# Layer norm without scale or shift: GpSimd's twelve first tiles written as six in a loop, with a semaphore for each operation

## The chip, the cores and the metric

The kernel runs on one core of a Trainium2 chip. The metric is the device time of one execution in microseconds (us). The span of the trace, from the first to the last instruction, is about 2 us shorter than that time; the difference is called "outside the span". All runs shown are in the fast state, on one core with a granted clock of 1.0.

## The reference

```python
# x: 32 x 512 x 1024 float32, eps = 1e-5
mean = np.mean(x, axis=-1, keepdims=True)
var = np.var(x, axis=-1, keepdims=True)
return ((x - mean) / np.sqrt(var + eps)).astype(np.float32)
```

There are 16,384 rows of 1024 elements: 67.11 MB are read and 67.11 MB are written.

## The kernel before

Rows are taken in 17 tiles. A tile has 128 partitions with 8 rows each (4 MiB); the last two have 6 and 2 rows. Six tiles fit into a ring in SBUF. For each tile, four engines hand on to each other:

1. SyncE loads the tile, once the store of the tile six places earlier has freed the slot.
2. VectorE computes statistics (`bn_stats`, 16 instructions for a tile) and raises `taken`.
3. GpSimd merges them in nine small operations into a sum of squares.
4. ScalarE takes the root. VectorE takes the reciprocal of the root. GpSimd multiplies mean and reciprocal.
5. ScalarE normalizes the eight rows in place and issues the store.

VectorE's program and GpSimd's, before:

```python
    def vector(t, arrived, turn):
        K, row, at = plan[t]
        for k in range(K):
            for s in range(NSUB):
                i = nc.vector.bn_stats(...)                    # cut: operands
                if k == 0 and s == 0:
                    i._wait_ge(landed[t], arrived)
                # cut: tile 0 comes in two halves; a wait for the second
        i.then_inc(taken, 1)
        if t >= len(plan) - LAST:                              # LAST = 2
            return
        nc.vector.reciprocal(
            out=rstd[:, at : at + K], in_=std[:, at : at + K]
        )._wait_ge(rooted[t], turn).then_inc(inverse, 1)
    # tiles 0 to 2, then two turns of a loop of six tiles, then the rest

    def gp(i, sem, value):
        nonlocal npool
        i._wait_ge(sem, value).then_inc(pool, 1)
        npool += 1
        return pool, npool

    for t, (K, row, at) in enumerate(plan):
        n = gp(g.tensor_tensor(out=h, in0=mean4[:, :, 0:2], in1=mean4[:, :, 2:4], op=ALU.add), taken, t + 1)
        n = gp(g.tensor_tensor(out=nm, in0=h[:, :, 0], in1=h[:, :, 1], op=ALU.add), *n)
        n = gp(g.tensor_scalar(out=nm, in0=nm, scalar1=-1.0 / H, scalar2=None, op0=ALU.mult), *n)
        # cut: six more, each waiting for the one before it
        if t < len(plan) - LAST:
            n = inverse, t + 1
        else:
            n = gp(g.tensor_tensor(..., op=ALU.pow), rooted[t], 1)
        ready.append(gp(g.tensor_mul(out=nmr[:, at : at + K], in0=nm, in1=rstd[:, at : at + K]), *n))
```

Note the order on VectorE: statistics of tile t, then the reciprocal of tile t, then the statistics of tile t+1. The reciprocal waits for GpSimd and ScalarE.

## Time and profile before

| | before |
|---|---|
| time, median of the first 3 runs | 318.22 us (318.08 to 318.25) |
| span of the profiled run | 315.8 us |
| busy: VectorE, ScalarE, GpSimd | 50%, 48%, 13% |
| bytes moved, rate over the span | 134.2 MB, 425 GB/s |

In the profile, PE, DVE, ACT, POOL and SP are the tensor, vector, scalar, GpSimd and sync engines; L118 is a line of the kernel. In lists in order of time the columns are start, duration, engine, line, operation, out<-in, count; the bracket gives the idle time ahead and what ended it. The slices are 40 equal parts of the span, each digit a busy share in tenths. The lines themselves are in the prediction.

### The profile page before, as it was taken

To read this page: it belongs to the slowest core of one execution; us is meant where nothing else is said; L and a number is where in the kernel's file an instruction comes from. 1 tells how busy PE (TensorE), PEld (TensorE's weight loads), DVE (VectorE), ACT (ScalarE), POOL (GpSimd) and SP (SyncE) were. 2 spreads that over 40 slices of the span, in tenths; PEclk is the share of its full clock that TensorE was granted. 3 is DMA by queue.
4 is the path that set the end of the run, shared out by engine and by line. 5 is a ranking of instruction groups with operands and counts; after the bars stand their busy time and mean duration, and the time that the engine had idled before them with its cause. 6 is when DMAs were issued, how large, how long until landed. Compare 5 with 4: busy or idle time off the path is not lost.

```text
span 315.8 us, 695 instructions
## 1 busy us (share of the span) xinstructions
DVE 156.4 (50%) x273; ACT 153.0 (48%) x146; POOL 41.7 (13%) x176
## 2 busy tenths in 40 slices
DVE  0396595865190752908438093470925619193000
ACT  1006595865925609165190742907438083474700
POOL 0002202022002020020201102011020200205200
DMA  7999999999999999999999999999999999999996
GB/s 299 432 465 398 448 398 415 453 411 452 412 449 415 444 419 452 415 452 415 452 415 448 423 440 432 432 436 432 440 423 440 423 438 432 423 431 447 419 436 295
DMA packets 5044, 134.24 MB, mean 425 GB/s; under 512 B 561, under 2 KB 561, under 8 KB 561
## 3 DMA queue, kind: packets, MB, share of 16 engines
q10 hardware_dynamic: 2592, 69.21, 51.0%
q1 hardware_dynamic: 2448, 65.01, 48.0%
q14 instruction: 4, 0.02, 0.0%
HBM read 67.11 MB, written 67.11 MB: 425 GB/s over the span
## 4 chain that ended last, share of the span: by engine, by line
DMA 61%; DVE 18%; ACT 9%; POOL 5%; issue 2%; ACTq 0%; DVEq 0%; SPq 0%
DMA ring<-in_x_dram 31%; DMA out_dram<-ring 29%; DVE stats L118 17%; ACT ring L228 9%; ACT std L218 1%; POOL rstd L198 1%; POOL dev L179 1%; POOL dev L184 1%; POOL dev L172 0%; POOL dev L177 0%; POOL nmean L168 0%; POOL half L162 0%; POOL half L185 0%; POOL nmean L166 0%; POOL ss L188 0%
## 5 line engine op out<-in xcount | busy, mean ns | idle before, releaser
L118 DVE BATCH_NORM_STATS2 stats<-ring 128x6 f32<-128x512 f32 x256 | 153.4, 677 | 85.4 <-DMA ring<-in_x_dram 84.8
L228 ACT ACTIVATE ring<-ring,nmr,rstd 128x1024 f32<-128x1024 f32 x128 | 146.6, 1226 | 11.2 <-POOL nmr L209 11.2
L218 ACT ACTIVATE std<-ss,eps_t 128x8 f32<-128x8 f32 (+2 forms) x17 | 5.1, 300 | 134.4 <-POOL ss L188 134.0
L162 POOL TENSOR_TENSOR half<-stats 128x16 f32<-128x16 f32 (+2 forms) x17 | 4.0, 234 | 231.6 <-DVE stats L118 231.6
L129 DVE RECIPROCAL rstd<-std 128x8 f32<-128x8 f32 x15 | 3.0, 203 | 48.5 <-ACT std L218 48.5
L179 POOL TENSOR_SCALAR dev<-dev 128x32 f32<-128x32 f32 (+2 forms) x17 | 5.0, 295 | 1.5
L209 POOL TENSOR_TENSOR nmr<-nmean,rstd 128x8 f32<-128x8 f32 (+2 forms) x17 | 3.5, 205 | 9.9 <-DVE rstd L129 9.7
L184 POOL TENSOR_TENSOR dev<-dev,stats 128x32 f32<-128x32 f32 (+2 forms) x17 | 4.3, 255 | 1.4
L172 POOL TENSOR_TENSOR dev<-stats,nmean 128x32 f32<-128x32 f32 (+2 forms) x17 | 4.1, 241 | 1.4
L177 POOL TENSOR_TENSOR dev<-dev 128x32 f32<-128x32 f32 (+2 forms) x17 | 4.0, 238 | 1.3
L168 POOL TENSOR_SCALAR nmean<-nmean 128x8 f32<-128x8 f32 (+2 forms) x17 | 4.0, 235 | 1.5
L185 POOL TENSOR_TENSOR half<-dev 128x16 f32<-128x16 f32 (+2 forms) x17 | 3.7, 215 | 1.3
L166 POOL TENSOR_TENSOR nmean<-half 128x8 f32<-128x8 f32 (+2 forms) x17 | 3.4, 202 | 1.3
L188 POOL TENSOR_TENSOR ss<-half 128x8 f32<-128x8 f32 (+2 forms) x17 | 3.4, 201 | 1.3
L198 POOL TENSOR_TENSOR rstd<-std,power 128x6 f32<-128x6 f32 (+1 forms) x2 | 2.1, 1041 | 3.0 <-ACT std L218 3.0
L218 ACT ACT_TABLE_LOAD x1 | 1.3, 1283 | 1.3 <-SPq L54 1.3
L133 DVE MEMSET eps_t<- 128x1 f32 x1 | 0.1, 59 | 1.0 <-SPq L54 1.0
L264 POOL MEMSET const-float32-0.0<- 128x1 f32 x1 | 0.1, 99 | 0.2 <-issue 0.2
L264 POOL MEMSET const-bfloat16-1.0<- 128x1 bf16 x1 | 0.1, 102 | 0.0
L264 POOL MEMSET const-uint8-127<- 128x1 uint8 x1 | 0.1, 102 | 0.0
L264 POOL MEMSET const-float32-1.0<- 128x1 f32 x1 | 0.1, 99 | 0.0
L134 DVE MEMSET power<- 128x8 f32 x1 | 0.1, 65 | 0.0
## 6 DMA issues: line engine op xcount, KB each, us to landing
out_dram<-ring ACTq DMA_DIRECT2D x15, 4096.0 KB, 47.4
ring<-in_x_dram SPq DMA_DIRECT2D x14, 4096.0 KB, 44.4
ring<-in_x_dram SPq DMA_DIRECT2D x1, 3072.0 KB, 42.0
out_dram<-ring ACTq DMA_DIRECT2D x1, 3072.0 KB, 16.5
ring<-in_x_dram ACTq DMA_DIRECT2D x1, 2048.0 KB, 12.2
ring<-in_x_dram SPq DMA_DIRECT2D x1, 2048.0 KB, 12.4
ring<-in_x_dram SPq DMA_DIRECT2D x1, 1024.0 KB, 53.8
out_dram<-ring ACTq DMA_DIRECT2D x1, 1024.0 KB, 14.8
```

The costliest lines, as they stand in the source:

```text
L118: i = nc.vector.bn_stats(out=stats[:, at + k, s, :], in_=ring[:, at + k, s * BN_MAX : (s + 1) * BN_MAX],)
L162: g.tensor_tensor(out=h, in0=mean4[:, :, 0:2], in1=mean4[:, :, 2:4], op=ALU.add),
L168: g.tensor_scalar(out=nm, in0=nm, scalar1=-1.0 / H, scalar2=None, op0=ALU.mult),
L172: g.tensor_tensor(out=d, in0=mean4, in1=nm.unsqueeze(2).to_broadcast([P, K, H]), op=ALU.add),
L177: n = gp(g.tensor_mul(out=d, in0=d, in1=d), *n)
L179: g.tensor_scalar(out=d, in0=d, scalar1=float(D // H), scalar2=None, op0=ALU.mult),
L184: n = gp(g.tensor_tensor(out=d, in0=d, in1=m2, op=ALU.add), *n)
L185: n = gp(g.tensor_tensor(out=h, in0=d[:, :, 0:2], in1=d[:, :, 2:4], op=ALU.add), *n)
L198: g.tensor_tensor(out=rstd[:, at : at + K], in0=std[:, at : at + K], in1=power[:, :K], op=ALU.pow,),
L209: g.tensor_mul(out=nmr[:, at : at + K], in0=nm, in1=rstd[:, at : at + K]),
L218: nc.scalar.activation(out=std[:, at : at + K], in_=ss[:, at : at + K], func=AF.Sqrt, bias=eps_t[:], scale=1.0 / D,)._wait_ge(*summed[t]). ...
L228: i = nc.scalar.activation(out=ring[:, k, :], in_=ring[:, k, :], func=AF.Identity, bias=nmr[:, k : k + 1], scale=rstd[:, k : k + 1],).then ...
```

## The change

The intent is a shorter program for GpSimd: tiles 0 to 5 are written once and run twice, and tiles 12 to 16 follow unrolled. A wait in a loop needs a value that holds in each turn. One semaphore that counts all operations does not give it simply, so each operation has its own, which rises by one per tile, and a register holds the tile's number.

```diff
-    taken, inverse, pool, act = map(
-        nc.alloc_semaphore, ("taken", "inverse", "pool", "act")
-    )
+    taken, inverse, act = map(nc.alloc_semaphore, ("taken", "inverse", "act"))
+
+    steps = [nc.alloc_semaphore(f"step_{i}") for i in range(11)]
 ... (cut)
-    for t, (K, row, at) in enumerate(plan):
+    def combine(t, count):
 ... (cut)
+        before = taken
+        def then(step, i, other=None):
+            nonlocal before
+            i._wait_ge(before, count) if other is None else i._wait_ge(*other)
+            before = steps[step]
+            i.then_inc(before, 1)
+
+        then(0, g.tensor_tensor(out=h, in0=mean4[:, :, 0:2], in1=mean4[:, :, 2:4], op=ALU.add))
 ... (cut: the same ten operations, eleven on the last two tiles)
+    count = g.alloc_register("count")
+    g.reg_mov(count, 1)
+    with g.Fori(0, TURNS):
+        for t in range(SLOTS):
+            combine(t, count)
+            g.reg_add(count, count, 1)
+    for t in range(TURNS * SLOTS, len(plan)):
+        combine(t, t + 1)
+    summed = [(steps[8], t + 1) for t in range(len(plan))]
+    ready = [(steps[10], t + 1) for t in range(len(plan))]
```

By my listing of the two programs, GpSimd goes from 183 instructions to 131.

More of the change, by code (lines that the diff above doesn't have):

```diff
@@ L145 @@
         vector(t, 16, 1)
-    npool, summed, ready = 0, [], []
-    def gp(i, sem, value):
-        nonlocal npool
-        i._wait_ge(sem, value).then_inc(pool, 1)
-        npool += 1
-        return pool, npool
     g = nc.gpsimd
-    for t, (K, row, at) in enumerate(plan):
+    def combine(t, count):
+        K, row, at = plan[t]
         parts = stats[:, at : at + K].rearrange("p g s (h c) -> p g (s h) c", h=2)
@@ L160 @@
         nm, d, h = nmean[:, at : at + K], dev[:, :K], half[:, :K]
-        n = gp(
-            g.tensor_tensor(out=h, in0=mean4[:, :, 0:2], in1=mean4[:, :, 2:4], op=ALU.add),
-            taken,
-            t + 1,
-        )
-        n = gp(g.tensor_tensor(out=nm, in0=h[:, :, 0], in1=h[:, :, 1], op=ALU.add), *n)
-        n = gp(
-            g.tensor_scalar(out=nm, in0=nm, scalar1=-1.0 / H, scalar2=None, op0=ALU.mult),
-            *n,
-        )
-        n = gp(
-            g.tensor_tensor(
-                out=d, in0=mean4, in1=nm.unsqueeze(2).to_broadcast([P, K, H]), op=ALU.add
-            ),
-            *n,
-        )
-        n = gp(g.tensor_mul(out=d, in0=d, in1=d), *n)
-        n = gp(
+        s2, r, std_t = ss[:, at : at + K], rstd[:, at : at + K], std[:, at : at + K]
+        before = taken
[5 more added lines that the diff above has]
+        then(0, g.tensor_tensor(out=h, in0=mean4[:, :, 0:2], in1=mean4[:, :, 2:4], op=ALU.add))
+        then(1, g.tensor_tensor(out=nm, in0=h[:, :, 0], in1=h[:, :, 1], op=ALU.add))
+        then(
+            2,
+            g.tensor_scalar(out=nm, in0=nm, scalar1=-1.0 / H, scalar2=None, op0=ALU.mult),
+        )
+        spread = nm.unsqueeze(2).to_broadcast([P, K, H])
+        then(3, g.tensor_tensor(out=d, in0=mean4, in1=spread, op=ALU.add))
+        then(4, g.tensor_mul(out=d, in0=d, in1=d))
+        then(
+            5,
             g.tensor_scalar(
@@ L181 @@
             ),
-            *n,
         )
-        n = gp(g.tensor_tensor(out=d, in0=d, in1=m2, op=ALU.add), *n)
-        n = gp(g.tensor_tensor(out=h, in0=d[:, :, 0:2], in1=d[:, :, 2:4], op=ALU.add), *n)
-        summed.append(
-            gp(
-                g.tensor_tensor(
-                    out=ss[:, at : at + K], in0=h[:, :, 0], in1=h[:, :, 1], op=ALU.add
-                ),
-                *n,
-            )
-        )
+        then(6, g.tensor_tensor(out=d, in0=d, in1=m2, op=ALU.add))
+        then(7, g.tensor_tensor(out=h, in0=d[:, :, 0:2], in1=d[:, :, 2:4], op=ALU.add))
+        then(8, g.tensor_tensor(out=s2, in0=h[:, :, 0], in1=h[:, :, 1], op=ALU.add))
         if t < len(plan) - LAST:
-            n = inverse, t + 1
+            own = inverse, count
         else:
-            n = gp(
-                g.tensor_tensor(
-                    out=rstd[:, at : at + K],
-                    in0=std[:, at : at + K],
-                    in1=power[:, :K],
-                    op=ALU.pow,
-                ),
-                rooted[t],
-                1,
-            )
-        ready.append(
-            gp(
-                g.tensor_mul(
-                    out=nmr[:, at : at + K], in0=nm, in1=rstd[:, at : at + K]
-                ),
-                *n,
-            )
-        )
+            i = g.tensor_tensor(out=r, in0=std_t, in1=power[:, :K], op=ALU.pow)
+            then(9, i, (rooted[t], 1))
+            own = steps[9], t - (len(plan) - LAST) + 1
+        then(10, g.tensor_mul(out=nmr[:, at : at + K], in0=nm, in1=r), own)
+    count = g.alloc_register("count")
[8 more added lines that the diff above has]
+    ready = [(steps[10], t + 1) for t in range(len(plan))]
     for t, (K, row, at) in enumerate(plan):
```

## The prediction

The six parts are 0 us each, and the sum is 318.22 + 0 = 318.2 us. The 0.005 for a faster result is the author's estimate alone.

> **What bounds the kernel now.** I read the page first: the busy shares of the engines, then the slices, then the DMA totals and issues.
>
> ```profile
> DVE 156.4 (50%) x273; ACT 153.0 (48%) x146; POOL 41.7 (13%) x176
> ...
> DMA  7999999999999999999999999999999999999996
> ...
> q14 instruction: 4, 0.02, 0.0%
> HBM read 67.11 MB, written 67.11 MB: 425 GB/s over the span
> ...
> out_dram<-ring ACTq DMA_DIRECT2D x15, 4096.0 KB, 47.4
> ring<-in_x_dram SPq DMA_DIRECT2D x14, 4096.0 KB, 44.4
> ```
>
> What to see: no engine is above 50%, and the sixteen DMA engines are at 90% or more in 38 of 40 slices; only the first and the last are lower (7 and 6 tenths). So 134.2 MB of transfers set the time, and GpSimd, which the change is about, is at 13%. The last two rows show how deep the transfers queue: a 4 MiB store takes 47.4 us from issue to landing, a load 44.4 us.
>
> Next, the Vector engine in order of time, for the pace of the steady part:
>
> ```profile
> 85.53 9.59 DVE L118 BATCH_NORM_STATS2 stats<-ring 128x6 f32<-128x512 f32 x16 [6.34 <-DMA ring<-in_x_dram]
> 98.36 0.20 DVE L129 RECIPROCAL rstd<-std 128x8 f32<-128x8 f32 x1 [3.24 <-ACT std L218]
> 104.89 9.59 DVE L118 BATCH_NORM_STATS2 stats<-ring 128x6 f32<-128x512 f32 x16 [6.33 <-DMA ring<-in_x_dram]
> ```
>
> A tile takes 104.89 - 85.53 = 19.36 us, and in each VectorE sits 6.3 us waiting for the next load. One tile is a load and a store of 4.19 MB each: 8.39 MB / 19.36 us = 433 GB/s. GpSimd's own waits, and the one in front of tile 6, say the same from its side:
>
> ```profile
> POOL half L162 <- DVE stats L118: 231.6, 17, 22.6
> ...
> 114.56 0.23 POOL L162 TENSOR_TENSOR half<-stats 128x16 f32<-128x16 f32 x1 [15.72 <-DVE stats L118]
> ```
>
> GpSimd waits 231.6 of 315.8 us for statistics. The chain of waits does pass through it, but look at what carries the chain: 61% of it is DMA, 5% POOL, and the two DMA pieces in a row are the whole latency of a queue, not of one transfer.
>
> ```profile
> 66.06 9.17 ACT ring L228 x8
> 75.23 0.02 issue
> 75.25 43.33 DMA out_dram<-ring
> 118.58 0.02 issue
> 118.60 44.36 DMA ring<-in_x_dram
> ```
>
> **The slack of a GpSimd delay.** This is the number that decides, so I work it out. With loads and stores sharing 433 GB/s, one 4.19 MB transfer moves in about 19.4 us (estimate: 4.19 MB at half of 433). The store above took 43.33 us and the load 44.36 us, so each stood some 24 us in a queue behind others. A store that is issued later by d us therefore waits d us less in the queue, as long as d stays under about 24 us; the DMA engines do not notice. The ring closes the same way: 9.6 (statistics) + 3.6 (GpSimd, root, reciprocal, last multiply) + 9.2 (ACT) + 43.3 + 44.4 is 110 us on this path, against six tiles of 19.36 = 116 us, and most of both DMA terms is queueing.
>
> [...]
> - [...] the new code keeps a wait at each step, only on a semaphore of its own. In the trace each such wait shows as 0.07 to 0.08 us of issue between two GpSimd pieces of the chain.
> - [...] The trace has a loop already, on VectorE; going into it left 0.6 us of idle in all (moves, an alignment, branches)[...].
> - [...] the page of before shows what fetches cost in any case: 4 packets, 0.02 MB, 0.0% of the engines.
>
> **The change, part by part.** By the listing of both programs GpSimd goes from 183 instructions to 131 (tiles 0 to 5 written once and run twice, tiles 6 to 11 gone, tiles 12 to 16 as they were). Other engines keep theirs in the same order; only the semaphore names on ACT's two waits per tile change. What GpSimd executes on data is unchanged: the same 10 operations on each of 15 tiles and 11 on each of the last two.
>
> 1. *Removed:* 60 instructions of code [...], no executed work. [...] 0 us.
> 2. *Waits.* For 12 tiles the value comes from a register instead of a constant. VectorE has the same change inside one run, between its reciprocals ahead of the loop (constant) and in it (register):
>
> ```profile
> 39.02 0.02 issue
> 39.04 0.20 DVE rstd L129
> ...
> 65.52 0.02 issue
> 65.54 0.21 DVE rstd L129
> ```
>
> Both waits end 0.02 us after the releaser, so a register costs nothing to see there. For GpSimd I take 0; if it were 0.1 us for each of 10 waits, that is 1 us a tile, against 24 us of slack.
> 3. *Counter:* one register addition a tile. VectorE's sequencer pieces in its loop entry last 0.04 us each; 12 x 0.04 = 0.5 us in all, behind the last multiply of a tile, where GpSimd next waits 9 to 16 us for statistics. On the path: 0.
> 4. *Entry, one branch back, one exit.* By VectorE's entry some 0.6 us each. The entry lies in the first 22.6 us, in which GpSimd waits for tile 0. The branch back lies after tile 5's last multiply, in the 15.72 us shown above. The exit lies after tile 11, in an equal gap. On the path: 0.
> 5. *Semaphores:* one (`pool`) becomes eleven, each counted by one operation alone. More names, the same number of increments: 0.
> 6. *Start and tail.* The first store is issued at 35.85 us; until then 25.2 MB of loads for six slots are queued, some 58 us of DMA work at 433 GB/s, so a delay of the first tiles is hidden too. Tiles 15 and 16 end the program and are outside the loop, with constants as before.
>
> Sum on the path that sets the end: 0 us. 318.22 + 0 = **318.2 us**.
>
> **Rivals.**
> - *GpSimd gets slow enough to starve the stores.* It would need about 24 us more per looped tile, on an engine that works 2.4 us on one (41.7 / 17). A register wait would have to cost over 2 us. Speaking for it: nothing in this trace shows a register wait on GpSimd itself. Against: VectorE's 0.02 us. If it happened, each of 12 tiles would add its excess over the slack, and the time would go to 330 us or more. I give it 1%.
> - *The smaller program saves time* (fewer instruction fetches among saturated queues, or less to do around the span). For: the time of the profiled run is 318.03 and its span 315.8, so 2.2 us lie outside it, and instructions are fetched by the same DMA engines. Against: four packets in a whole span. It could give 0.1 to 0.3 us, far under 2%.
> [...]
> - *The order of loads and stores in the queues shifts*, since stores are issued slightly later. The bytes and the rate stay; it moves the end by tenths of a us in either direction. This sets my range.
>
> **Range and chances.** The three runs of before lie within 0.17 us, the profiled one at 318.03. I allow four times that spread each way for another order in the queues and another build: 317.5 to 318.9. Two per cent is 6.4 us; only the first rival makes that, so slower has 0.01. Faster by 6.4 us would need 134.2 MB in under 309.6 us of span, 434 GB/s on average with the fill and drain included[...]: 0.005.
>
> **What would show it.** Right: DMA slices all 9 but the ends, tiles still 19.36 us apart on VectorE, GpSimd's operations with the same means (about 0.2 to 0.3 us), idle before `half` still ended by the statistics. Step 2 shows in the issue gaps between GpSimd pieces of looped tiles (0.07 us if free) against those of tiles 12 to 16; steps 3 and 4 in a first operation of a tile that starts later than 0.07 us after the last statistics; step 1 in the instruction queue's packets. The prediction is wrong if VectorE's 6.3 us waits for loads shrink or vanish in the loop, or if a slice of DMA in the middle falls under 9.

## The result

| | before | after |
|---|---|---|
| median of 6 runs each | 318.24 us (318.08 to 318.44) | 317.77 us (317.60 to 318.24) |
| ratio after / before | | 0.9986, 95% interval 0.9973 to 0.9999 |
| span | 315.8 us (profiled run) | 315.8 to 316.4 us (6 runs) |
| outside the span | 2.2 us (profiled run) | 1.80 to 1.88 us (6 runs) |

The ratio is the mean time of one kernel's fast runs over that of the other's of the same rounds, so it is not quite the ratio of the medians. The difference is 0.14%. The two spans are alike: what difference there is lies outside.

The page of the kernel after, in the lines that answer to those of before (busy shares, DMA slices, instruction queue, bytes):

```profile
DVE 156.4 (49%) x273; ACT 153.0 (48%) x146; POOL 41.7 (13%) x176
...
DMA  7999999999999999999999999999999999999996
...
q14 instruction: 3, 0.02, 0.0%
HBM read 67.11 MB, written 67.11 MB: 425 GB/s over the span
```

The DMA slices are the same, digit for digit, and GpSimd is busy for the same 41.7 us with the same 176 instructions that count as work. The instruction queue has 3 packets against 4 in the span, but this is no saving: by the records of the two traces, three packets of 8,192 bytes fall within the span in both, and the fourth of before has 24 bytes and stands at 0.02 us.

VectorE's statistics of tiles 5 and 6 after, and GpSimd's first operation on tile 6, which is the first after the branch back:

```profile
86.32 9.59 DVE L119 BATCH_NORM_STATS2 stats<-ring 128x6 f32<-128x512 f32 x16 [6.35 <-DMA ring<-in_x_dram]
105.66 9.59 DVE L119 BATCH_NORM_STATS2 stats<-ring 128x6 f32<-128x512 f32 x16 [6.30 <-DMA ring<-in_x_dram]
```

```profile
115.33 0.23 POOL L166 TENSOR_TENSOR half<-stats 128x16 f32<-128x16 f32 x1 [15.69 <-DVE stats L119]
```

A tile takes 105.66 - 86.32 = 19.34 us (19.36 before), and VectorE still waits 6.3 us for each load. The statistics of tile 6 end at 105.66 + 9.59 = 115.25 us, and GpSimd starts 0.08 us later; before, it was 114.56 - 114.48 = 0.08 us as well. So the branch back is hidden in the 15.69 us of idle time: its record stands at 99.48 us, and two short `MODIFY_POOL_CONFIG` records at the head of the loop, which the second turn runs again, are over at 99.83 us. The record of this branch is 0.05 us long, that of the exit after tile 11 0.04 us. No packet of the instruction queue starts between 94.3 us and the end of the span, so no fetch shows for the branch either.

The end of the chain's passage through GpSimd on tile 3, after:

```profile
65.34 0.07 issue
65.41 0.20 POOL ss L183
65.61 0.61 issue
66.23 0.03 POOLq L197
66.26 0.00 issue
66.26 0.21 POOL nmr L190
```

The gap ahead of an operation that waits on the register's value is 0.07 us, what it was with a constant. The counter's addition is the piece of 0.03 us on GpSimd's sequencer (`POOLq`; 0.05 us on tile 0). It stands ahead of the last multiply in time, although it comes after it in the program: it starts 0.04 us after the end of the reciprocal for which the multiply waits, and the multiply starts 0.08 us after that end, on the twelve tiles with an addition as on tiles 12 to 14 without one. The multiply starts 0.65 us after the last sum (66.26 - 65.61), as before (65.82 - 65.17). So the addition costs nothing either.

### The profile page after: what moved, and what is told of

It is laid out like the page before. It is cut to its first block, busy times and chain, and to the rows that moved or that the text cites. A ratio compares the mean times of both kernels' runs of the same rounds, so it can differ in the third digit from the quotient of the medians.

```text
span 316.0 us, 713 instructions
## 1 busy us (share of the span) xinstructions
DVE 156.4 (49%) x273; ACT 153.0 (48%) x146; POOL 41.7 (13%) x176
## 4 chain that ended last, share of the span: by engine, by line
DMA 61%; DVE 18%; ACT 9%; POOL 5%; issue 2%; ACTq 0%; DVEq 0%; POOLq 0%; SPq 0%
DMA ring<-in_x_dram 32%; DMA out_dram<-ring 29%; DVE stats L119 17%; ACT ring L215 9%; POOL rstd L187 1%; POOL dev L177 1%; POOL dev L181 1%; ACT std L205 0%; POOL dev L173 0%; POOL nmean L170 0%; POOL dev L174 0%; POOL half L166 0%; POOL half L182 0%; POOL nmean L167 0%; POOL ss L183 0%
```

## The experiments

Two questions were open. First: 0.47 us between the medians is small, but is it real, and where does it come from? Second: the prediction rests on a slack of 24 us for a delay on GpSimd. The result does not test that, since the change brought no delay to hide.

### Why 0.4 us less?

The changed kernel's own loop has a scalar multiplication that waits on a register. To keep clear of that form of instruction, in the experiments the two scalar multiplications are `tensor_tensor` with constant tiles. VectorE fills these in two more memsets. All outputs were correct.

**r1_loop** is the changed kernel so rewritten:

```diff
-        then(2, g.tensor_scalar(out=nm, in0=nm, scalar1=-1.0 / H, scalar2=None, op0=ALU.mult))
+        then(2, g.tensor_tensor(out=nm, in0=nm, in1=minus[:, :K], op=ALU.mult))
 ... (cut)
-        then(5, g.tensor_scalar(out=d, in0=d, scalar1=float(D // H), scalar2=None, op0=ALU.mult))
+        then(5, g.tensor_tensor(out=d, in0=d, in1=wide[:, :K], op=ALU.mult))
```

> The loop with the two scalar multiplications of GpSimd as tensor_tensor with a constant tile (131 GpSimd instructions, as in the change). Theory 'less code': 0.3 to 0.5 us under the kernel before (about 317.8 against 318.24), with a span that is equal within 0.2 us, so the gain lies outside the span (some 1.8 us outside instead of 2.2) and one 8 KB instruction packet fewer after the end. Theory 'noise or another order in the queues': within 0.2 us of before, the part outside the span at 2.2 us. Either way the gaps between GpSimd operations stay 0.07 to 0.08 us.

**r2_unrolled** is r1_loop without the loop:

```diff
-    with g.Fori(0, TURNS): ... (cut)
+    for t in range(len(plan)):
+        combine(t, t + 1)
```

> The same with its eleven semaphores but all 17 tiles written out (183 GpSimd instructions, as before). Theory 'less code': equal to before within 0.15 us, 2.2 us outside the span. Theory 'the separate semaphores are what gains': about 317.8, like the loop.

**r3_loop_pad** is r1_loop and **r4_before_pad** the kernel before, with 52 and 128 memsets of one column ahead of GpSimd's work:

```diff
+    for i in range(52):                                  # 128 in r4_before_pad
+        nc.gpsimd.memset(pad[:, i : i + 1], 0.0)
```

> The loop with 52 small memsets ahead of it on GpSimd, in its first idle 22 us, so that the program has 183 GpSimd instructions again. Theory 'less code': the gain is gone, about 318.2, 2.2 us outside the span. Theory 'it is the loop itself': about 317.8.

> The kernel before with 128 small memsets ahead of GpSimd's work [...]. Theory 'less code, step by instruction packet': 0.3 to 0.5 us slower than before, outside the span. Theory 'only a fixed boundary that the change went under': equal to before within 0.15 us. In no case is the span more than 0.3 us longer, since the memsets run in GpSimd's first idle 22 us.

These four ran on one chip with five rounds. Their numbers are in the table below. The loop repeats the result (317.77 us against 318.17, ratio 0.9988, interval 0.9975 to 1.0002), and the part outside the span, which varies by at most 0.09 us between the runs of a kernel (spans are recorded to 0.1 us), tells where: 1.79 to 1.87 us against 2.19 to 2.27, with mean spans of 315.94 and 315.93 us. The separate semaphores are not the cause: r2_unrolled has them and 2.20 to 2.26 us outside.

Nor is it the amount of code, which I had expected. r3_loop_pad has as many instructions as before by the listing (one more by the trace) and still 1.82 to 1.87 us outside. r4_before_pad has 128 more and no more outside than before (2.17 to 2.20). A delay experiment that is told further down, d5_late, gave a hint: 195 unrolled GpSimd instructions and 1.77 to 1.86 us outside. In the traces of before and after, the large packets of the instruction queue have 8,192 bytes. So the next idea was that the place counts where GpSimd's program ends within such a packet.

**e2_before_pad12** and **e3_before_pad76** are the kernel before with 12 and 76 of these memsets. That makes 195 instructions, as in d5_late, and 259, which is 128 more than the changed kernel has. How many instructions fill a packet no trace shows; that programs 128 apart end at the same place in one was the author's assumption:

> The kernel before with 12 small memsets in GpSimd's first idle time: 195 GpSimd instructions, as many as d5_late has. The time outside the span was 1.8 us in d5_late and 2.2 us in before. Theory 'where GpSimd's program ends in its 8 KB instruction packets decides' (P): 1.8 us outside, so about 317.8. Theory 'it is the late work itself, or the loop' (W): 2.2 us outside, 318.2.

> With 76 memsets: 259 GpSimd instructions[...]. Theory P: 1.8 us outside the span, about 317.8, though the program is the longer. Theory W or 'less code': 2.2 us or more outside, 318.2.

**e4_pow_pad** puts 125 of them into p0_pow (below), in which VectorE's program is shorter too, and has 323, again 128 more than d5_late:

> The kernel p0_pow (198 GpSimd instructions, 2.2 us outside) with 125 memsets: 323[...]. Theory P: 1.8 us outside the span. If VectorE's program, shorter here by its reciprocals, decides as well: 2.2 us.

| kernel | loop on GpSimd | GpSimd instructions | median, us | mean span, us | outside, us |
|---|---|---|---|---|---|
| before (of r1 to r4) | no | 183 | 318.17 | 315.93 | 2.19 to 2.27 |
| after | yes | 131 | 317.77 | 315.98 | 1.80 to 1.88 |
| r1_loop | yes | 131 | 317.77 | 315.94 | 1.79 to 1.87 |
| r2_unrolled | no | 183 | 318.30 | 316.12 | 2.20 to 2.26 |
| r3_loop_pad | yes | 183 | 317.95 | 316.20 | 1.82 to 1.87 |
| r4_before_pad | no | 311 | 318.27 | 316.08 | 2.17 to 2.20 |
| e2_before_pad12 | no | 195 | 317.92 | 316.10 | 1.80 to 1.85 |
| e3_before_pad76 | no | 259 | 317.80 | 316.05 | 1.77 to 1.85 |
| d5_late | no | 195 | 317.97 | 316.07 | 1.77 to 1.86 |
| p0_pow (VectorE shorter) | no | 198 | 318.20 | 316.00 | 2.15 to 2.24 |
| e4_pow_pad (VectorE shorter) | no | 323 | 318.76 | 316.60 | 2.15 to 2.24 |

The part outside the span takes one of two values 0.4 us apart. Two experiments say that the amount of code is not what chooses between them: e3_before_pad76 has 76 instructions more than before and is on the lower value, and r4_before_pad with 52 more than that is on the higher one. With the other engines' programs as they were and without a loop on GpSimd, 183 and 311 instructions give 2.2 us, 195 and 259 give 1.8 us, as expected. e1_late8 and d10_late, with the 195 of d5_late (and, like it, two more memsets on VectorE), have 1.82 to 1.86 and 1.79 to 1.84 us. The 183 and 311 are 128 apart, and so are the changed kernel's 131 and the 259. That is all that speaks for a place within a packet; these are only four lengths without a loop, and that the packet is the cause is not shown. But the same 0.4 us can be had by adding twelve idle memsets.

What this account does not cover stays open. r3_loop_pad has the 183 of before by the listing and 1.85 us. It may be that a loop moves something; but by the trace its program is one instruction longer than that of before (197 records against 196, the loop counted once), and no kernel without a loop was tried between 183 and 195, so the border may lie between the two. e4_pow_pad is 128 longer than the 195 of d5_late and has 2.2 us (and, unexplained, a span 0.6 us longer than before). There VectorE's program is shorter too, as in p0_pow and p10_pow_late (2.14 to 2.23 us outside), and whether its end counts too was not tried alone. What the core does in these 0.4 us no trace shows: the records of instructions stop at the end of the span. The packets of 8,192 bytes that come after it don't settle it. In the profiled runs there is one in every kernel that has the lower value, r3_loop_pad excepted. There are two in before, r2_unrolled and r4_before_pad, which have the higher; but r3_loop_pad, with the lower, has two as well, and the three kernels with the shorter VectorE program have the higher with none.

### How much delay does the kernel hide?

Two accounts stand against each other. **Q**, the prediction's: a delay on GpSimd is hidden as long as transfers wait in their queues, some 24 us. **V**: VectorE takes tile t's reciprocal ahead of tile t+1's statistics. So a delay of GpSimd goes straight into VectorE's cycle, which is 12.90 us (the statistics of tiles 1 and 2 start at 26.26 and 39.16 us in the trace of before). Then only 19.36 - 12.90 = 6.5 us a tile are free.

**d5_late**, **e1_late8** and **d10_late** put one slow operation ahead of GpSimd's ten on tiles 0 to 11, the twelve tiles that the change loops over. Its width sets its length (5.45, 8.05 and 10.58 us at 32, 48 and 64 elements a row):

```diff
+    DELAY = 32                                           # 48 in e1_late8, 64 in d10_late
 ... (cut: three tiles of this width, two memsets on VectorE)
+        n = taken, t + 1
+        if t < 12:
+            n = gp(g.tensor_tensor(out=lost[:], in0=base[:], in1=down[:], op=ALU.pow), *n)
         n = gp(
             g.tensor_tensor(out=h, in0=mean4[:, :, 0:2], in1=mean4[:, :, 2:4], op=ALU.add),
-            taken,
-            t + 1,
+            *n,
         )
```

> The kernel before with one slow power operation (about 5.4 us, estimate from 730 ns for 2 and 1352 ns for 6 elements a row) ahead of GpSimd's ten on tiles 0 to 11. Theory Q (what I wrote: a delay is hidden up to the 24 us that a transfer queues): 318.2, same. Theory V (VectorE waits for each tile's root before the next tile's statistics, so the delay adds to its 12.9 us a tile, and only the 6.3 us that it waits for loads are free): 18.3 us a tile is under 19.36, so also same, with VectorE's waits for loads down to about 1 us.

> The same with about 10.3 us. Theory Q: 318.2, same. Theory V: a tile takes VectorE 12.9 + 10.3 = 23.2 us instead of 19.36, tile 12's statistics start at about 13 + 12 x 23.2 = 292 us instead of 221, then five tiles to go: about 360 us (350 to 370), DMA slices under 9 in the middle, no wait of VectorE for loads in the looped tiles.

> The kernel before with a power operation of about 8.0 us (between the two measured, 5.45 us for 32 and 10.58 us for 48 more... 64 elements a row) ahead of GpSimd's ten on tiles 0 to 11. Theory V (VectorE's own order is the bound above 6.35 us): a tile takes 12.9 + 8.1 = 21.0 us, 1.7 us over the DMA's 19.36, times 12 tiles is 20 us: 338 to 340 us. If the step from 5.4 to 10.3 us had another cause (a queue that runs dry all at once), it could be anywhere from 318 to 370.

**p0_pow** takes VectorE out of the circle. GpSimd computes the reciprocal of every tile, as it did for the last two:

```diff
-LAST = 2
+LAST = 17
 ... (cut)
-                1,
+                sixteens(rooted, t) // 16,
```

> The kernel before with the reciprocal of every tile on GpSimd (as its last two tiles have it), so VectorE never waits for GpSimd. No delay. Both theories: same, 318.2 within 0.7, GpSimd busy some 1.6 us more a tile; VectorE waits for loads some 9.7 us a tile (19.36 - 9.6).

**p10_pow_late** is p0_pow with the delay of d10_late:

> The kernel p0_pow with the 10.3 us operation on tiles 0 to 11. Theory Q, now with VectorE out of the cycle: 318.2, same, since GpSimd's own 10.3 + 2.4 + 1.7 and its waits of about 1 us are 15.4 us a tile, under 19.36, and the latency of 10.3 us is under 24 us of queueing. If a delay costs whatever VectorE does (theory L, latency itself counts): some 10 us or more slower. Theory V holds only if d10_late is slow and this one isn't.

| kernel | delay a tile | VectorE in the circle | time, us (median) | before beside it | ratio, 95% interval |
|---|---|---|---|---|---|
| d5_late | 5.45 us | yes | 317.97 | 318.22 | 0.9990 (0.9973 to 1.0006) |
| e1_late8 | 8.05 us | yes | 339.11 | 318.24 | 1.0657 (1.0639 to 1.0674) |
| d10_late | 10.58 us | yes | 369.82 | 318.22 | 1.1620 (1.1600 to 1.1639) |
| p0_pow | none | no | 318.20 | 318.22 | 0.9999 (0.9982 to 1.0015) |
| p10_pow_late | 10.55 us | no | 319.48 | 318.22 | 1.0045 (1.0028 to 1.0062) |

Account Q falls: 8 us, a third of the 24, already cost 21 us. d5_late alone would not tell the accounts apart, since both expected no change. VectorE in order of time in d5_late:

```profile
142.94 0.20 DVE L133 RECIPROCAL rstd<-std 128x8 f32<-128x8 f32 x1 [8.76 <-ACT std L226]
143.06 9.54 DVE L122 BATCH_NORM_STATS2 stats<-ring 128x6 f32<-128x512 f32 x16
161.37 0.20 DVE L133 RECIPROCAL rstd<-std 128x8 f32<-128x8 f32 x1 [8.77 <-ACT std L226]
161.49 9.54 DVE L122 BATCH_NORM_STATS2 stats<-ring 128x6 f32<-128x512 f32 x16
```

The waits for loads are gone; VectorE runs from one wait for its root (8.77 us, before 3.23) to the next. A tile takes it 161.49 - 143.06 = 18.43 us, which is 12.90 + 5.45 + 0.08. That is under 19.36 us, and the DMA slices are those of before, so the DMA engines still set the end and the time doesn't move. About 1 us of wait for loads was expected to be left; VectorE has none and runs ahead of the 19.36 us, so the vanishing of this wait is not yet a loss. The queues do get shallower: the median store takes 28.0 us to land instead of 47.4.

In d10_late:

```profile
155.47 9.54 DVE L122 BATCH_NORM_STATS2 stats<-ring 128x6 f32<-128x512 f32 x16
178.90 0.20 DVE L133 RECIPROCAL rstd<-std 128x8 f32<-128x8 f32 x1 [13.89 <-ACT std L226]
179.02 9.54 DVE L122 BATCH_NORM_STATS2 stats<-ring 128x6 f32<-128x512 f32 x16
```

Now it is 23.55 us a tile, 4.19 over the DMA's pace. Twelve tiles make 50.3 us, and the means differ by 369.77 - 318.25 = 51.5 us; the spans differ by 51.9 us, since the part outside is 0.4 us shorter here. Of the 1.6 us that remain in the span, some 0.9 us are VectorE's own loop: its entry and its branch back, hidden before in the waits for loads, now lie on the path (two of the starts are 24.2 and 23.8 us apart instead of 23.55). e1_late8 confirms the slope that this gives: 21.02 us a tile, 12 x 1.66 = 19.9 us, with 20.9 measured; the expectation was 338 to 340 us. A straight line through the two costs reaches zero at a delay of 6.3 us, close to the 6.5 us of account V. For d10_late I had expected about 360 (350 to 370), ten too low, because I took a shorter tail and a shorter delay than the run has.

The page of d10_late shows what the bound looks like from the DMA side (busy shares, DMA slices, bytes):

```profile
DVE 155.1 (42%) x275; ACT 153.1 (42%) x146; POOL 168.6 (46%) x188
...
DMA  8999999999997989979889898998979906677697
...
HBM read 67.11 MB, written 67.11 MB: 365 GB/s over the span
```

No engine is over 46% and the DMA slices have holes: what binds is the order of waits between two engines, not the work of either. The busiest engine is GpSimd with its 46%, idle for over half of the time, and the DMA moves 365 GB/s where 433 have been reached, so neither figure alone shows this bound.

p10_pow_late is the control. The same delay of 10.55 us, with VectorE free of GpSimd, costs 1.3 us instead of 51.5. VectorE there again waits 9.8 us for each load in the steady part:

```profile
136.21 9.59 DVE L122 BATCH_NORM_STATS2 stats<-ring 128x6 f32<-128x512 f32 x16 [9.76 <-DMA ring<-in_x_dram]
155.58 9.59 DVE L122 BATCH_NORM_STATS2 stats<-ring 128x6 f32<-128x512 f32 x16 [9.77 <-DMA ring<-in_x_dram]
```

So a delay in latency of that size is hidden by the queues, as the prediction had it, but here only where VectorE does not wait for GpSimd in its own order. Whether it holds up to 24 us was not tried. Where the 1.3 us come from can be placed, not explained. In stretches of the span (busy times by engine, then clock, DMA share and GB/s), the rows from 40 to 160 us of p10_pow_late and of p0_pow, the same kernel without the delay, are

```profile
40.00:80.00 40.00, 27.37 (x47) 27.07 (x26) 37.56 (x25) 1.00 1.01 425
80.00:160.00 80.00, 37.13 (x63) 47.30 (x45) 73.73 (x63) 1.00 1.00 428
```

```profile
40.00:80.00 40.00, 21.45 (x36) 29.46 (x28) 12.05 (x34) 1.00 1.00 425
80.00:160.00 80.00, 38.37 (x64) 40.39 (x40) 16.01 (x44) 1.00 1.01 434
```

From 80 to 160 us the DMA engines are as busy, and move 6 GB/s less: 80 us x 6 GB/s = 0.48 MB, or 1.1 us at 433 GB/s. From 40 to 80 us the rate is the same, and in the three other stretches up to 280 us it is within 1 GB/s. Why the rate is lower there was not tried.

No experiment points to a version that beats both kernels by more than the 0.4 us outside the span: from 80 to 240 us both kernels move 432 to 433 GB/s, and no stretch of 40 us or more that was read moves more than 434.

## Why the prediction was right, and where it was not

- **The bound, and the sum of 0 us on the path: right.** Spans before and after are equal within their scatter (315.7 to 316.4 us), the DMA slices are the same, and the pace is 19.34 against 19.36 us. The time of 317.77 lies in the range of 317.5 to 318.9.
- **Waits on a register (step 2): right.** The gaps on GpSimd are 0.07 us as before.
- **Counter, entry and branch back (steps 3 and 4): right.** The addition shows as 0.03 us and the multiply starts 0.08 us after the reciprocal with it and without. The first operation of tile 6 starts 0.08 us after the statistics in both kernels.
- **The separate semaphores (step 5): right**, shown by r2_unrolled.
- **The smaller program (step 1 and the second rival): the place was right, the cause was not.** I allowed 0.1 to 0.3 us outside the span, against a sum of 0. It is 0.4 us, outside the span, but it does not come from there being less code: 259 instructions have the lower value and 183 the higher. My count of 4 instruction packets in the span was misread as well: one of them has 24 bytes, and both kernels have three of 8,192. The range was drawn for another order in the queues, of which the spans show nothing; that it also took in the 0.4 us outside the span was luck.
- **The slack (the part "The slack of a GpSimd delay", and the first rival): wrong.** I wrote that a later store waits that much less in the queue "as long as d stays under about 24 us", and that GpSimd would need "about 24 us more per looped tile" to starve the stores. The free time is 6.5 us a tile: 5.45 us cost nothing and 8.05 us cost 20.9 us. The working took a delay for a matter of one tile's latency and left out that VectorE doesn't begin the next tile until it has this one's reciprocal. The line that shows it stood in the prediction: VectorE's own wait of 6.3 us for a load is the slack of everything in its cycle. My last sentence even named its vanishing as the sign of trouble, yet without drawing the number from it. The conclusion held in spite of the step, and that was luck of a kind: the change brought no delay at all, and even my worst case of 1 us a tile for the waits happened to be under 6.5 us.

## What to carry to other kernels

Ask of a delay not only how much latency the queues hide, but which engine waits for it in its own order before it may take the next tile: the free time is that engine's wait for input per tile, here 6.5 us, not the 24 us of queueing. Here, a shorter program on an engine that mostly waits (GpSimd, busy 13%) saved nothing of its own; a gain of some tenths of a us should be split into span and rest before it is credited to the change, and tried against a few idle instructions in the old kernel.
